# Decode states of a hybrid decoder step, stepped four tokens a unit and multiplied in eight pieces of four tokens

## The chip, the core and the metric

The kernel runs on one core of one Trainium2 chip. The metric is device time in microseconds (us) of one execution, the median of several. Of the core's engines, TensorE (PE in the profile, with its weight loads as PEld) does all matrix products, VectorE (DVE) and ScalarE (ACT) do elementwise work and empty PSUM, GpSimd (POOL) mostly issues the stores, and SyncE (SP) issues the loads. In the trace each engine's instructions come in the order of its own list; an instruction whose operand isn't ready holds what stands behind it there.

## The reference

One layer, with a prompt of 1024 tokens and eight decode tokens (`DEC_BATCH = 8`, one new token each). Both go through one input projection, then an RG-LRU group and an mLSTM group with four heads, then the output projection and a norm. What the change touches is the mLSTM of the decode tokens. For one decode token b and head h, with a state matrix C of 256 x 256 in float32:

```python
num = (jnp.einsum('bhts,bshv->bthv', P, v)
       + ginter.transpose(0, 2, 1)[..., None] * jnp.einsum('bthk,bhkv->bthv', q, C))
...
decay = jnp.exp(b[:, :, -1:] - b + igh - mL[:, :, None])
carry_scale = jnp.exp(b[:, :, -1] + m - mL)
C_new = carry_scale[..., None, None] * C + jnp.einsum('bhs,bshk,bshv->bhkv', decay, k, v)
```

So each of the 32 states (8 tokens x 4 heads, 256 KB each) is read, scaled by one number, given a rank-one update k v^T, and written out as an output. The kernel multiplies the token's query with the updated state (q C), and that product goes on into the token's output row.

## The kernel before

**The projection and its units.** The input projection is worked in 14 units of two blocks of 256 weight columns each (`UNITS`, unit 0 = `v0v1` to unit 13 = `z2z3`). A unit's two blocks against the two halves of the prompt make a 2 x 2 block product, which is done with seven products instead of eight (P1, P2, P5, P6, P7, P4, P3, by the names in the code), and each product in two halves. That makes 14 **parts** a unit. A part is twelve matmuls of 512 columns or twenty-four of 256, always in threes (`mm3`, lines 66 to 68: high x high, low x high, high x low of numbers that were split into a high and a low float32r part; the split is line 72 on ACT and line 73 on DVE). The weights of a product are prepared two products ahead of their use (`LEAD = 2`). Units 1 to 13 run from about 76 us to 667 us of the span; the output projection follows.

**The decode rows of a unit.** The decode tokens need the same projection. `dec_unit(u)` does it in float32 with eight matmuls (line 256) whose stationary operand is 32 columns wide; four of them stand side by side in the array, each at its own 32 columns (`pz[32 * g:32 * g + 32, :]`). It is issued where unit u's product P5 is prepared, which is just ahead of the unit's first part. ACT copies the result out (line 259), and a transposition follows later (line 264).

**The decode states.** When a head's q, k and v are there, its steps are queued in `dcq`: `first`, then `token(0)` to `token(7)`. A token's step scales its state on ACT (line 992), adds the rank-one update with two DVE instructions (line 994), has POOL store the state (line 996), and asks SP for the next token's v (line 965) and for later states (line 971). There are four state buffers (`Cb`, `bufs=4`). After each second token, `products` is put off by two parts (two passes through the `late` list) and then issues four matmuls for the two tokens: two halves of the state, two tokens, four 32-column places side by side in one PSUM bank (line 1013). These use a stationary operand of 32 columns for the first two tokens of a head (`qfirst`) and of 4 columns for the others (`qsel`). After the last two tokens DVE copies the bank (line 1019), and a small matmul pair (line 1024) sorts the rows.

**What sets the order.** After each part the loop calls `pop_bg`, which runs what is due in `late`, then takes a step each from the background work (`bg`), the RG-LRU steps (`rgq`), and, only at some parts, the decode steps (`dcq`). Before, that was each third part up to unit 9, and each second part from unit 10. The framework then orders the instructions of each engine itself: an instruction whose operands it reckons ready earlier can be put ahead of ones that the program lists first. So ACT's scaling of a state, which needs only the loaded state, often stands well ahead of the step's place in the loop. When the decode steps and all other background work are done after unit 9, the first blocks of the prompt's mLSTM (`m_first`) begin to be taken from `bg`.

Of the kernel before, what the change touches and what calls it, by code (L numbers as in the profile page):

```python
# [20 lines left out]
NB = 8  # L21
# [21 lines left out]

UNITS = "v0v1 x0y0 q0k0 x1y1 q1k1 x2y2 v2v3 q2k2 x3y3 q3k3 o0o1 o2o3 z0z1 z2z3".split()
NWS, NSTG, LEAD = 6, 7, 2
DEC = 10, 2, 3
RQ = [Q_P1, Q_P2, Q_P5, Q_P6, Q_P7, Q_P4, Q_P3]
NR, NZ = 28, 4

# [2 lines left out]
def hymba_kernel(  # L52
# [181 lines left out]
    def load_raw(u, b, parts=(0, 1)):  # L234
# [5 lines left out]
        for a in parts:  # L240
# [7 lines left out]
               "z": lambda j: dz[:, 2 * j:2 * j + 2], "x": lambda j: dxz[:, 0, 2 * j:2 * j + 2],  # L248
               "y": lambda j: dxz[:, 1, 2 * j:2 * j + 2]}

    def dec_unit(u):

        pz = ps("tr" if u < 2 else "o", [P, 512])
        for k in range(KC):
            g = k % 4
            TE.matmul(pz[32 * g:32 * g + 32, :], hnd[:, NB * k:NB * k + 32], raws[u, k // 4][:, k % 4, :], start=k < 4, stop=k >= 4,  # L256
                      skip_group_check=True)
        Z = sg([P, 512], "Z")
        A.copy(Z, pz)

        def turn():
            pt = ps("tr", [P, 4, P]) if u < 2 else pz.rearrange("p (m q) -> p m q", m=4)
            for m in range(4):
                TE.transpose(pt[:, m, :], Z[:, m * P:(m + 1) * P], idF)  # L264
            for a, (kind, j) in enumerate(units[u]):
                src = pt[:, 2 * a:2 * a + 2].rearrange("p m (g b) -> p m b g", g=4)[:, :, 0:NB, :]
                V.tensor_reduce(dec_dst[kind](j), src, axis=mybir.AxisListType.X, op=ALU.add)
                if kind == "k":
                    V.tensor_scalar(dec_dst[kind](j), dec_dst[kind](j), 1.0 / 16.0, None, op0=ALU.mult)
        late.append(turn if u < 2 else lambda: late.append(turn))  # L270
# [678 lines left out]

    def dec_open():  # L950
        p2 = fpr["p"]
        fetch_C(0)
        fetch_C(1)

        fpr["qsel"] = qsel = p2.tile([P, 2, 36], F32, tag="qsel", name="qsel")
        G.memset(qsel, 0.0)
        fpr["qfirst"] = qfirst = p2.tile([P, 2, 2, 32], F32, tag="qfirst", name="qfirst")
        G.memset(qfirst, 0.0)
        fpr["selq"] = selq = p2.tile([P, NB], F32, tag="selq", name="selq")
        idq = idF.rearrange("p (r k m) -> p r k m", r=2, k=2)  # L960
        V.tensor_tensor(selq.rearrange("p (m r) -> p r m", r=2), idq[:, :, 0, 0:4], idq[:, :, 1, 0:4], op=ALU.add)
# [11 lines left out]
    def decode_steps(h):  # L973

        p2 = fpr["p"]
        qsel, qfirst, selq = fpr["qsel"], fpr["qfirst"], fpr["selq"]
        st = {}

        def first():
            st["kw"] = kw = p2.tile([P, 2, NB], F32, tag="kw", name="kw")  # L980
            V.tensor_tensor(kw, dk[:, 2 * h:2 * h + 2, :], dW[:, :, h].unsqueeze(1).to_broadcast([P, 2, NB]), op=ALU.mult)
            V.tensor_copy(qsel.rearrange("p k (m r) -> p k m r", r=9)[:, :, :, 0:5:4],
                          dq[:, 2 * h:2 * h + 2, :].rearrange("p k (m r) -> p k m r", r=2))
            V.tensor_copy(qfirst[:, :, :, 0], dq[:, 2 * h:2 * h + 2, 0:2])
            fetch_v(h, 0)

        def token(b):
            i = h * NB + b

            def f():  # L990
                vb_, C = ds_.pop(("v", i)), ds_["C", i]
                A.mul(C, C, dGI[:, b, h:h + 1])
                for kb in range(2):
                    V.scalar_tensor_tensor(C[:, kb, :], vb_, st["kw"][:, kb, b:b + 1], C[:, kb, :],
                                           op0=ALU.mult, op1=ALU.add)
                stq(s_C[0, b, h].rearrange("(kb p) v -> p kb v", p=P), C)
                if b + 1 < NB:
                    fetch_v(h, b + 1)
                if b % 2:
                    late.append(lambda: late.append(products))  # L1000
                else:
                    fetch_C(i + 2)
                    fetch_C(i + 3)


            def products():
                if b == 1:
                    st["pq"] = ps("qp", [P, 512])
                pq = st["pq"]
                for g in range(4):  # L1010
                    bb, kb = b - 1 + g // 2, g % 2
                    q, n = (qfirst[:, kb, bb, :], 32) if b == 1 else (qsel[:, kb, 4 * bb:4 * bb + 4], 4)
                    TE.matmul(pq[32 * g:32 * g + n, 0:256], q, ds_["C", h * NB + bb][:, kb, :], start=b == 1,  # L1013
                              stop=b == NB - 1, skip_group_check=True)
                for bb in (b - 1, b):
                    del ds_["C", h * NB + bb]
                if b == NB - 1:
                    Z = sg([P, 256], "qC")
                    V.tensor_copy(Z, pq[:, 0:256])

                    def turn():
                        pt = pq[:, 256:272].rearrange("p (v b) -> p v b", v=2)
                        for vb in range(2):
                            TE.matmul(pt[:, vb, :], Z[:, vb * P:(vb + 1) * P], selq, start=True, stop=True)
                        V.tensor_copy(dqC[:, 2 * h:2 * h + 2, :], pt)
                    late.append(lambda: late.append(turn))
            return f
        return [first] + [token(b) for b in range(NB)]


    def bh(t):
# [660 lines left out]
    for n, (u, q) in enumerate(seq):  # L1692
        preps(n + 1 + LEAD)
        for _ in product(u, q):
            pop_bg(2 if u == 1 or u == last_u else 1, 1, part % DEC[1 if u >= DEC[0] else 2] == 1)
            part += 1
        if u == last_u:
            wo_due(q)
        if q == 6:
            for kind, j in units[u]:  # L1700
                if kind == "x":
                    rg_unit(j)
            for half in range(2):
                if u == max(unit_of["v", 2 * half], unit_of["v", 2 * half + 1], 1):
                    bg.append(lambda half=half: dec_rows(half))
            for h in range(NH):
                if done_h[h] == u:
                    bg.append(lambda h=h: dcq.extend(decode_steps(h)))
            if u == last_u - 1:
                dgen = decode_outputs()  # L1710

                def step():
                    next(dgen, None)
                    run_late()
                state["out"] = [step] * 5 + [m_open2]
        if not state["m"] and u > max(done_h) and not (bg or rgq or dcq or late):
            m_start()
        if u == last_u and q == 0:
            if not state["m"]:
                while bg or rgq or dcq or late:  # L1720
                    pop_bg()
                m_start()
            bg.extend(state["out"])
# [105 lines left out]
```

## Time and profile before

| what | value |
|---|---|
| time, median of 3 runs | 916.23 us (916.17 to 916.24) |
| profiled execution: span from first to last instruction | 913.5 us |
| median of the runs less that span | 2.7 us |
| PE busy / PEld / DVE / ACT / POOL | 902.1 / 749.2 / 741.5 / 590.1 / 194.2 us |
| mean granted TensorE clock | 0.998 |
| decode-row passes, line 256 | 224, in 14 groups of 16 |
| state-product passes, line 1013 | 128, in 16 groups of 8, first at 186.6 us, last at 538.0 us |

A float32 matmul stands in the trace as two passes, so eight matmuls are 16 rows there and four are 8. The profile gives only the span as the profiled execution's own time; what lies outside (2.7 us) is the launch and the end. In the timeline a row has its start, its length, engine, line, operation, output and inputs, tile shape, and a count. A matmul's length contains its way through the array and overlaps with its neighbours', so the cost of a stretch of TensorE work is read from starts, not from lengths.

### The profile page before, as it was taken

Reading aid. Unit: us, or ns where it says so; the run is one execution under the profiler, and the core shown is the slowest. Engines: PE = TensorE matmul, PEld = TensorE weight load, DVE = VectorE, ACT = ScalarE, POOL = GpSimd, SP = SyncE. Lnnn points to the kernel's source line nnn. Section 1 sums busy time; section 2 is a strip of 40 time slices with the busy share of each in tenths; the row PEclk is TensorE's granted clock in tenths of the full one; section 3 lists DMA queues with packets and bytes.
Section 4 is the critical chain, followed back from the end, with each engine's and each line's share of the span. In section 5 each row is a group of like instructions: output and inputs, shape, how many; then the busy total and the mean of one; then the engine's idle time right before and its main releaser. Section 6 shows DMA issues by size and latency. Waiting matters only on the chain.

```text
span 913.5 us, 15513 instructions
## 1 busy us (share of the span) xinstructions
PE 902.1 (99%) x5259; PEld 749.2 (82%) x5259; DVE 741.5 (81%) x1532; ACT 590.1 (65%) x1086; POOL 194.2 (21%) x322
## 2 busy tenths in 40 slices
PE   8999999999999999999999999999999999999996
PEld 6897777877787988787789898877788888888886
DVE  6874788978689878789888786679998879888973
ACT  7663446867567776577658786446786568566642
POOL 1111113112312222324332334010111111121120
PEclk9999999999999999999999999999999999999999
DMA  6611457455746566548665747345789889846531
GB/s 202 193 62 46 138 170 243 134 201 186 229 152 212 165 198 198 192 144 265 202 237 167 266 139 243 108 132 188 217 230 260 201 206 300 225 138 183 181 123 68
DMA packets 130488, 167.68 MB, mean 184 GB/s; under 512 B 17596, under 2 KB 98564, under 8 KB 130402
## 3 DMA queue, kind: packets, MB, share of 16 engines
q1 hardware_dynamic: 108790, 103.68, 37.4%
q0 software_dynamic: 21616, 63.02, 21.0%
q8 instruction: 41, 0.67, 0.3%
q14 instruction: 37, 0.30, 0.1%
q10 hardware_dynamic: 4, 0.00, 0.0%
HBM read 108.00 MB, written 62.92 MB: 187 GB/s over the span
## 4 chain that ended last, share of the span: by engine, by line
PE 97%; ACT 1%; DVE 1%; DMA 0%; issue 0%; POOL 0%; ACTq 0%; POOLq 0%
PE ps_o L66 16%; PE ps_o L68 15%; PE ps_o L67 15%; PE ps_kv L66 12%; PE ps_kv L68 11%; PE ps_kv L67 11%; PE ps_o L256 2%; PE ps_s L1195 2%; PE ps_qp L1013 1%; PE ps_s L824 1%; PE ps_tr L824 1%; PE ps_qp L67 1%; PE ps_qp L66 1%; PE ps_qp L68 1%; PE ps_s L1197 1%; PE ps_o L264 1%
## 5 line engine op out<-in xcount | busy, mean ns | idle before, releaser
L72 ACT CAST wh<-raw 128x1024 fp32r<-128x1024 f32 x91 | 95.4, 1049 | 77.9 <-PE ps_o L67 19.3
L73 DVE TENSOR_TENSOR wl<-raw,wh 128x1024 fp32r<-128x1024 f32 x91 | 111.0, 1220 | 34.9 <-ACT wh L72 19.8
L66 PE MATMUL ps_kv<-cb_hi,wh 128*128 128x512 f32 x320 | 127.3, 398 | 0.0
L68 PE MATMUL ps_kv<-cb_hi,wl 128*128 128x512 f32 x320 | 125.3, 392 | 0.0
L67 PE MATMUL ps_kv<-cb_lo,wh 128*128 128x512 f32 x320 | 125.0, 391 | 0.0
L66 PE MATMUL ps_o<-cb_hi,wh 128*128 128x512 f32 x240 | 95.2, 397 | 0.0
L68 PE MATMUL ps_o<-cb_hi,wl 128*128 128x512 f32 x240 | 93.7, 391 | 0.0
L67 PE MATMUL ps_o<-cb_lo,wh 128*128 128x512 f32 x240 | 93.6, 390 | 0.0
L66 PEld LDWEIGHTS ps_kv<-cb_hi,wh 128*128 128x128 f32 x320 | 60.1, 188 | 22.3 <-issue 4.6
L68 PEld LDWEIGHTS ps_kv<-cb_hi,wl 128*128 128x128 f32 x320 | 60.1, 188 | 13.0
L67 PEld LDWEIGHTS ps_kv<-cb_lo,wh 128*128 128x128 f32 x320 | 60.1, 188 | 12.7 <-issue 0.8
L66 PE MATMUL ps_kv<-wh,cb_hi 128*128 128x256 f32 x192 | 55.1, 287 | 0.0
L67 PE MATMUL ps_kv<-wl,cb_hi 128*128 128x256 f32 x192 | 54.4, 283 | 0.0
L68 PE MATMUL ps_kv<-wh,cb_lo 128*128 128x256 f32 x192 | 54.3, 283 | 0.0
L68 PEld LDWEIGHTS ps_o<-cb_hi,wl 128*128 128x128 f32 x240 | 45.1, 188 | 9.9
L66 PEld LDWEIGHTS ps_o<-cb_hi,wh 128*128 128x128 f32 x240 | 45.1, 188 | 9.7 <-issue 0.8
L66 PE MATMUL ps_o<-wo,mh 128*128 128x512 f32 (+1 forms) x136 | 53.0, 390 | 0.0
L67 PEld LDWEIGHTS ps_o<-cb_lo,wh 128*128 128x128 f32 x240 | 45.2, 188 | 8.9
L68 PE MATMUL ps_o<-wo,ml 128*128 128x512 f32 (+1 forms) x136 | 51.7, 380 | 0.0
L67 PE MATMUL ps_o<-wo,mh 128*128 128x512 f32 (+1 forms) x136 | 51.5, 379 | 0.0
L66 PE MATMUL ps_o<-wh,cb_hi 128*128 128x256 f32 x144 | 41.0, 285 | 0.0
L67 PE MATMUL ps_o<-wl,cb_hi 128*128 128x256 f32 x144 | 40.7, 283 | 0.0
(560 smaller groups left out, 2599.8 us busy)
## 6 DMA issues: line engine op xcount, KB each, us to landing
raw<-in_w_in_dram SPq DMA_DIRECT2D x55, 512.0 KB
Cb<-in_state_mlstm_C_dram SPq DMA_DIRECT2D x32, 256.0 KB
out_dram<-Cb POOLq DMA_DIRECT2D x32, 256.0 KB, 4.5
qk<-d_qk SPq DMA_DIRECT2D x32, 256.0 KB
ring<-d_ro SPq DMA_DIRECT2D x26, 256.0 KB
d_qk<-s POOLq DMA_DIRECT2D x24, 256.0 KB, 4.9
d_x<-s POOLq DMA_DIRECT2D x16, 256.0 KB, 2.8
zsr<-d_y SPq DMA_DIRECT2D x16, 256.0 KB
```

What stands on the lines that cost most here:

```text
L66: TE.matmul(out, ah, bh, start=first, stop=False, skip_group_check=True)
L67: TE.matmul(out, ah, bl, start=False, stop=False, skip_group_check=True)
L68: TE.matmul(out, al, bh, start=False, stop=last, skip_group_check=True)
L72: a = A.copy(hi, src)
L73: V.tensor_tensor(lo, src, hi.bitcast(F32), op=ALU.subtract)
L256: TE.matmul(pz[32 * g:32 * g + 32, :], hnd[:, NB * k:NB * k + 32], raws[u, k // 4][:, k % 4, :], start=k < 4, stop=k >= 4, skip_group_chec ...
L264: TE.transpose(pt[:, m, :], Z[:, m * P:(m + 1) * P], idF)
L824: TE.matmul(pg, w[:, n, :], st["xx"][n], start=k == 0, stop=k == 1)
L1013: TE.matmul(pq[32 * g:32 * g + n, 0:256], q, ds_["C", h * NB + bb][:, kb, :], start=b == 1, stop=b == NB - 1, skip_group_check=True)
L1195: TE.matmul(S, qk[:, 2 + kb, :], qk[:, kb, :], start=kb == 0, stop=kb == 1)
L1197: TE.transpose(kn[:, kb * P:(kb + 1) * P], qk[:, 2 + kb, :], idF)
```

## The change

Three things are changed together.

- **When the steps run.** The decode steps are taken at the parts 3, 5, 7, 9 and 11 of every unit (`DEC`), in place of each third or each second part. A head now takes two units: `first` and tokens 0 to 3 in one, an empty step and tokens 4 to 7 in the next.
- **When the products run.** They are issued for four tokens at a time, eight matmuls, eight times in all. After a group's fourth token, the group is put into a list `full`; the next `dec_unit` issues it right behind its own eight matmuls.
- **When the states are loaded.** Four states are fetched at the opening, and then four at a time, two parts after a group's products, into the same four buffers. Before, two were fetched at every second token.

```diff
-DEC = 10, 2, 3
+DEC = 3, 5, 7, 9, 11
...
+    full = deque()
+
     def dec_unit(u):
...
             TE.matmul(pz[32 * g:32 * g + 32, :], hnd[:, NB * k:NB * k + 32], raws[u, k // 4][:, k % 4, :], start=k < 4, stop=k >= 4,
                       skip_group_check=True)
+        if full:
+            full.popleft()()
         Z = sg([P, 512], "Z")
         A.copy(Z, pz)
...
-        fetch_C(0)
-        fetch_C(1)
+        for i in range(4):
+            fetch_C(i)
...
-                if b % 2:
-                    late.append(lambda: late.append(products))
-                else:
-                    fetch_C(i + 2)
-                    fetch_C(i + 3)
-
+                if b % 4 == 3:
+                    full.append(products)
 
             def products():
-                if b == 1:
+                if b == 3:
                     st["pq"] = ps("qp", [P, 512])
                 pq = st["pq"]
-                for g in range(4):
-                    bb, kb = b - 1 + g // 2, g % 2
...
+                for b0 in (b - 3, b - 1):
+                    for g in range(4):
+                        bb, kb = b0 + g // 2, g % 2
+                        q, n = (qfirst[:, kb, bb, :], 32) if b0 == 0 else (qsel[:, kb, 4 * bb:4 * bb + 4], 4)
+                        TE.matmul(pq[32 * g:32 * g + n, 0:256], q, ds_["C", h * NB + bb][:, kb, :], start=b0 == 0,
+                                  stop=b0 == NB - 2, skip_group_check=True)
+                for bb in range(b - 3, b + 1):
                     del ds_["C", h * NB + bb]
+                for n in (1, 3):
+                    late.append(lambda n=n: late.append(lambda: [fetch_C(i + n), fetch_C(i + n + 1)]))
...
-        return [first] + [token(b) for b in range(NB)]
+        steps = [token(b) for b in range(NB)]
+        return [first, *steps[:4], lambda: None, *steps[4:]]
...
-            pop_bg(2 if u == 1 or u == last_u else 1, 1, part % DEC[1 if u >= DEC[0] else 2] == 1)
+            pop_bg(2 if u == 1 or u == last_u else 1, 1, part % 14 in DEC)
```

**TensorE, the start of unit 4, before.** `raw0_4` and `raw1_4` are the unit's weights with the decode tokens as stationary operand (`hnd`); `ps_kv` is the first part's output.

```order
L256 MATMUL ps_o_2217<-raw0_4_1943,hnd_112 32x512 x4
L256 MATMUL ps_o_2217<-raw1_4_2057,hnd_112 32x512 x4
L66 MATMUL ps_kv_2234<-cb_hi0_187,wh4_0_2118 128x512
L67 MATMUL ps_kv_2234<-cb_lo0_188,wh4_0_2118 128x512
...
L68 MATMUL ps_kv_2234<-cb_hi0_187,wl4_0_2119 128x512
L1013 MATMUL ps_qp_2077<-Cb_1935,qsel_1374 4x256 x2
L1013 MATMUL ps_qp_2077<-Cb_1937,qsel_1374 4x256 x2
L66 MATMUL ps_kv_2260<-cb_hi0_187,wh4_0_2118 128x512
L67 MATMUL ps_kv_2260<-cb_lo0_188,wh4_0_2118 128x512
```

**The same place in the change.**

```order
L258 MATMUL ps_o_2208<-raw0_4_1937,hnd_112 32x512 x4
L258 MATMUL ps_o_2208<-raw1_4_2057,hnd_112 32x512 x4
L1014 MATMUL ps_qp_2217<-Cb_1370,qfirst_1380 32x256 x2
L1014 MATMUL ps_qp_2217<-Cb_1372,qfirst_1380 32x256 x2
L1014 MATMUL ps_qp_2217<-Cb_1374,qsel_1378 4x256 x2
L1014 MATMUL ps_qp_2217<-Cb_1376,qsel_1378 4x256 x2
L66 MATMUL ps_kv_2234<-cb_hi0_187,wh4_0_2109 128x512
L67 MATMUL ps_kv_2234<-cb_lo0_188,wh4_0_2109 128x512
```

The pieces that stood apart among the projection's matmuls are now one group behind the decode rows, with nothing between. The other seven groups stand the same way, behind the decode rows of units 5, 6, 7, 9, 10, 11 and 12.

**ACT, the start of unit 4, before.** `Z` is the copy of the decode rows, `s1` the copy of the first product's halves, `Cb` the scaling of a state, `wh4_3` and `wh4_4` high parts of the weights of later products.

```order
L259 COPY Z_2226<-ps_o_2217 128x512
L330 COPY s1_2247<-ps_kv_2234 128x512
L811 CAST xl_2284<-xc_2256 64x512
L992 ACTIVATE Cb_2294<-Cb_2294,dGI_110 128x512
L330 COPY s1_2273<-ps_kv_2260 128x512
L72 CAST wh4_3_2299<-raw0_4_1943 128x1024
L992 ACTIVATE Cb_2296<-Cb_2296,dGI_110 128x512
L72 CAST wh4_4_2345<-raw0_4_1943 128x1024
```

**The same place in the change.**

```order
L263 COPY Z_2226<-ps_o_2208 128x512
L334 COPY s1_2247<-ps_kv_2234 128x512
L815 CAST xl_2288<-xc_2252 64x512
L996 ACTIVATE Cb_2271<-Cb_2271,dGI_110 128x512
L996 ACTIVATE Cb_2273<-Cb_2273,dGI_110 128x512
L996 ACTIVATE Cb_2275<-Cb_2275,dGI_110 128x512
L334 COPY s1_2269<-ps_kv_2256 128x512
L72 CAST wh4_3_2293<-raw0_4_1937 128x1024
L996 ACTIVATE Cb_2277<-Cb_2277,dGI_110 128x512
L72 CAST wh4_4_2339<-raw0_4_1937 128x1024
```

Four scalings of states now stand close behind the decode rows, three of them ahead of the second `s1` copy. Their buffers are the ones that the products of the same unit have just read, so their loads can only be issued once those products are done.

**TensorE, unit 12, the prompt's first mLSTM block, in the change.** `ps_s<-qk` are its scores, `kh`, `vh`, `vl`, `ph` the operands that ACT and DVE make from them, `ps_o_6138` the projection's second half of P2.

```order
L1199 MATMUL ps_s_6009<-qk_5965 128x128 x2
L1201 MATMUL ps_s_6009<-idF_78,qk_5965 128x128 x2
L68 MATMUL ps_o_6138<-cb_hi1_189,wl12_1_5915 128x512
...
L66 MATMUL ps_qp_6098<-vh_5953,kh_6017 128x258
...
L66 MATMUL ps_s_6102<-vh_5953,kh_6017 128x258
...
L67 MATMUL ps_qp_6098<-vl_5954,kh_6017 128x258
...
L66 MATMUL ps_qp_6132<-vh_5953,ph_6015 128x258
...
L1199 MATMUL ps_s_6165<-qk_5971 128x128 x2
```

Before, the scores stood ahead of unit 12's decode rows, and 24 matmuls of the projection lay between them and the first use of `kh`. In the change the scores come some 40 rows later and five matmuls lie between. After this block the order of TensorE is the same as before to the end.

More of the change, by code (lines that the diff above doesn't have):

```diff
@@ L998, in f @@
                     fetch_v(h, b + 1)
-                if b % 2:
-                    late.append(lambda: late.append(products))
-                else:
-                    fetch_C(i + 2)
-                    fetch_C(i + 3)
+                if b % 4 == 3:
+                    full.append(products)
             def products():
-                if b == 1:
+                if b == 3:
                     st["pq"] = ps("qp", [P, 512])
                 pq = st["pq"]
-                for g in range(4):
-                    bb, kb = b - 1 + g // 2, g % 2
[L1012 to L1015, printed above, removed]
+                for b0 in (b - 3, b - 1):
[5 more added lines that the diff above has]
+                for bb in range(b - 3, b + 1):
                     del ds_["C", h * NB + bb]
+                for n in (1, 3):
+                    late.append(lambda n=n: late.append(lambda: [fetch_C(i + n), fetch_C(i + n + 1)]))
                 if b == NB - 1:
```

## The prediction

> **What bounds the kernel now.** I read the page first, then the table by stretches, TensorE's timeline around one group of the rows that the change moves, and last the waits.
>
> ```profile
> span 913.5 us, 15513 instructions
> PE 902.1 (99%) x5259; PEld 749.2 (82%) x5259; DVE 741.5 (81%) x1532; ACT 590.1 (65%) x1086; POOL 194.2 (21%) x322
> ```
> ```profile
> 112.00:612.00 500.00, 500.00 (x2911) 411.09 (x2913) 408.97 (x712) 336.07 (x498) 133.93 (x214) 1.00 0.59 190
> ```
>
> The second row is the stretch that holds all the work in question (units 2 to 13): PE is busy in 500 of 500 us at full clock, DVE in 409, ACT in 336, the DMA engines in 59% at 190 GB/s. A busy PE alone proves little, since the lengths of its rows overlap. So I look at starts.
>
> ```profile
> 205.63 0.40 PE L67 MATMUL ps_kv<-cb_lo,wh 128*128 128x512 f32 x1
> 205.87 0.39 PE L68 MATMUL ps_kv<-cb_hi,wl 128*128 128x512 f32 x1
> 206.10 0.40 PE L66 MATMUL ps_kv<-cb_hi,wh 128*128 128x512 f32 x1
> 206.33 0.39 PE L67 MATMUL ps_kv<-cb_lo,wh 128*128 128x512 f32 x1
> 206.56 0.39 PE L68 MATMUL ps_kv<-cb_hi,wl 128*128 128x512 f32 x1
> 206.88 0.61 PE L1013 MATMUL ps_qp<-Cb,qsel 128*4 128x256 f32 x8
> 207.43 0.50 PE L66 MATMUL ps_kv<-cb_hi,wh 128*128 128x512 f32 x1
> 207.76 0.39 PE L67 MATMUL ps_kv<-cb_lo,wh 128*128 128x512 f32 x1
> 207.99 0.40 PE L68 MATMUL ps_kv<-cb_hi,wl 128*128 128x512 f32 x1
> ```
>
> Full-size matmuls start every 0.23 us and nothing delays them; only around the product piece does the step widen, before it, behind it, and once more after the first full-size matmul. TensorE sets the time here, and each us of its stream saved is a us of span, as long as no other engine falls behind. [...]
>
> **The price of a piece.** From the last full-size start before (206.56) to the second one after (207.76) are 1.20 us; two steps would take 0.46. So this piece of two tokens costs 0.74 us. The same reading for a first piece of a head (32 columns) and for the decode rows of a unit:
>
> ```profile
> 186.32 0.39 PE L68 MATMUL ps_kv<-cb_hi,wl 128*128 128x512 f32 x1
> 186.64 0.64 PE L1013 MATMUL ps_qp<-Cb,qfirst 128*32 128x256 f32 x8
> 187.55 0.39 PE L67 MATMUL ps_kv<-cb_lo,wh 128*128 128x512 f32 x1
> ```
> ```profile
> 157.79 0.39 PE L68 MATMUL ps_kv<-cb_hi,wl 128*128 128x512 f32 x1
> 158.11 1.92 PE L256 MATMUL ps_o<-raw,hnd 128*32 128x512 f32 x16
> 159.96 0.50 PE L66 MATMUL ps_kv<-cb_hi,wh 128*128 128x512 f32 x1
> 160.30 0.40 PE L67 MATMUL ps_kv<-cb_lo,wh 128*128 128x512 f32 x1
> ```
>
> They cost 187.55 - 186.32 - 0.46 = 0.77 us and 160.30 - 157.79 - 0.46 = 2.05 us. Now both kinds run four passes side by side. A product piece is 8 passes of 256 columns, two rounds; the decode rows are 16 passes of 512 columns, four rounds of double length. With r for a round of 256 columns and s for going over to these narrow tiles and back: 2r + s = 0.74 and 8r + s = 2.05. So r = 0.218 us and **s = 0.30 us**. That s is the change of tile shape, and not of float32, is seen where one 128-wide float32 transposition stands inside the decode rows of unit 2:
>
> ```profile
> 115.20 0.39 PE L68 MATMUL ps_kv<-cb_hi,wl 128*128 128x512 f32 x1
> 115.52 1.06 PE L256 MATMUL ps_o<-raw,hnd 128*32 128x512 f32 x8
> 116.59 0.33 PE L701 MATMUL ps_qp<-idF,stk 128*128 128x128 f32 x1
> 116.85 1.06 PE L256 MATMUL ps_o<-raw,hnd 128*32 128x512 f32 x8
> 118.18 0.39 PE L67 MATMUL ps_kv<-cb_lo,wh 128*128 128x512 f32 x1
> ```
>
> This stretch costs 118.18 - 115.20 - 0.46 = 2.52 us, 0.47 more than the same rows without it, for a transposition of a quarter of the columns of a full-size matmul.
>
> **The sum on TensorE.**
>
> ```profile
> L1013 PE MATMUL ps_qp<-Cb,qsel x96: 379/379/380, 206.9 to 538.0; 128*4 128x256 f32 x96
> L1013 PE MATMUL ps_qp<-Cb,qfirst x32: 379/391/403, 186.6 to 497.4; 128*32 128x256 f32 x32
> ```
>
> - Removed: 12 pieces at 0.74 and 4 at 0.77, 11.96 us. Two of them stand directly ahead of another narrow or square float32 group and share the way back; I take off 0.15. Remains 11.8.
> - Added: 8 groups behind the decode rows. Each is 16 passes of 256 columns, four rounds: 4 x 0.218 = 0.87 us, with no s, because the decode rows have already paid it. The four with a `qfirst` take 0.03 more. Together 7.1 us.
> - Net: **-4.7 us**. The streaming is the same on both sides, 32 rounds; what goes is sixteen changes of shape and back, 16 x 0.30 = 4.8.
>
> What the trace doesn't hold is a round of narrow float32 tiles that follows a round on other data in another PSUM bank, nor one of 4 columns behind one of 32. Its bounds: nothing (as between rounds of one piece), and a full s at each of the eight seams, 8 x 0.30 = 2.4 us, which would leave -2.3. I take nothing: decode rows and pieces both start four passes at once, so both already work in the same four 32-column places. [...]
>
> **The other moved parts.** The scalings, updates, stores and loads of the 32 states stay in number; only their places change.
>
> - *Products waiting for their states.* TensorE now takes eight matmuls in a fixed place, and all of the projection is queued behind them. In DVE's order at least 24 rows lie between the last update of a group and the subtraction (line 285) that DVE does right behind the decode rows. By the stretch above a DVE row takes 409 / 712 = 0.57 us, so the updates are done some 13 us ahead; against that DVE runs a few us behind TensorE. I price it at nothing. Without that cover it would be up to a token's two updates, about 1 us, a group.
> - *ACT waiting for loads.* This is the wait that the change reshapes.
>
> ```profile
> ACT Cb L992 <- DMA Cb<-in_state_mlstm_C_dram: 22.8, 13, 3.5
> SPq L971 <- PE ps_qp L1013: 44.3, 11, 6.9
> ```
> ```profile
> 474.71 0.90 SPq L971 DMA_DIRECT2D Cb<-in_state_mlstm_C_dram  x2
> ```
> ```profile
> 480.96 0.72 ACT L992 ACTIVATE Cb<-Cb,dGI 128x512 f32<-128x512 f32 x1 [3.53 <-DMA Cb<-in_state_mlstm_C_dram]
> 481.58 0.57 ACT L330 COPY s<-ps_kv 128x512 f32<-128x512 f32 x1
> 482.05 1.04 ACT L72 CAST wh<-raw 128x1024 fp32r<-128x1024 f32 x1
> 483.00 0.72 ACT L992 ACTIVATE Cb<-Cb,dGI 128x512 f32<-128x512 f32 x1
> ```
>
> ACT waits 22.8 us in 13 places for states now, at worst 6.2 us after the issue (474.71 to 480.96), and the second state of that pair was there 8.3 us after it at the latest. TensorE had no gap there. In the change four states are asked for right behind the products, seven times (the first four come early). The 512 KB more take 2.8 us at 190 GB/s, so the fourth state lands at most L = 11 us after the products. Behind it on ACT stand its scaling (0.72), a copy (0.57) and a split (1.04), then DVE's half of that split (1.2, line 73 in the page):
>
> ```profile
> L73 DVE TENSOR_TENSOR wl<-raw,wh 128x1024 fp32r<-128x1024 f32 x91 | 111.0, 1220 | 34.9 <-ACT wh L72 19.8
> ```
>
> TensorE wants that weight for the fourth product, six parts of 12 x 0.23 = 2.76 us in, at 16.5 us. So L may be 16.5 - 3.5 = 13 us; at 11 two us are left. I price it at nothing.
> - *The prompt's first block.* It begins some ten us later in unit 12 and its chain (scores, ACT, DVE, products) has five matmuls, 1.15 us, as cover where it had 24. ACT's two pieces there take about 0.47 and 0.40 us:
>
> ```profile
> 560.41 0.40 ACT L72 CAST vh<-vt 128x256 fp32r<-128x256 f32 x1
> ...
> 564.62 0.47 ACT L1203 ACTIVATE kh<-ps_s,de_t 128x256 fp32r<-128x256 f32 x1
> ```
>
> They just fit. I put +0.2 us, between 0 and 1 (all of 0.87 in the open).
>
> Sum: -4.7 + 0.2 = -4.5 us. The span goes from 913.5 to about 909.0, and with the 2.7 us around it the time from 916.23 to **911.7 us**.
>
> **The rivals.**
>
> 1. *The seams cost a change of shape after all*, once a group: 8 x 0.30 = 2.4 us given back, 914.1 us. For it: 4-column tiles have never followed 32-column ones here. Against it: both start four at a time and overlap, which needs the same places.
> 2. *Side waits eat part of it*: in some units ACT or DVE is late by one or two us, or the prompt's block costs its full 1 us. 1 to 2.5 us in all, 912.7 to 914.2 us. For it: ACT's 3.5 us waits. Against: in 500 us of the present kernel they cost TensorE nothing.
> 3. *Nothing comes of it*, 916.2 us: TensorE's stream isn't the bound, or the saved changes are filled by waits that now show. DVE is next in line with 409 of the 500 us, 91 us of room against 4.5, so this needs waits, not work.
> 4. *Slower, by ACT.* Four loads in a burst land later than L = 13 us, ACT stands, and the fourth product's weights are late in each of the seven units: TensorE loses 7 x (L - 13). From L = 13.6 the gain is gone, from 13.9 the kernel is over 0.2% slower; at L = 14.5, 911.7 + 10.5 = 922 us. For it: all four share one SP queue with the weights of the next unit, and the stores of four states come in a burst too. Against: the slowest pair had 8.3 us at most.
>
> **How the numbers follow.** A measurement of this kernel can tell 0.2%, 1.8 us, from no change. Chances: the forecast 0.70, rival 1 0.10, rival 2 0.10, rival 3 0.06, rival 4 0.04. The forecast, rival 1 and nearly all of rival 2 lie under 914.4, so faster 0.87, same 0.09, slower 0.04. The range: at the low end the net sum with the present ACT waits gone where they might have cost something, -5.7, 910.5 us; at the high end the full price of the seams, 914.1, so that rivals 3 and 4 and a little more are left out.
>
> **What would show it.** In the profile of the changed kernel: line 1014 in 8 groups of 16 passes, each directly behind line 258, and from the last full-size start before such a pair to the second one behind it 2.05 + 0.87 + 0.46 = 3.4 us; with the seam's price it would be 3.7. TensorE busy without gaps from 112 us to 607. ACT's wait for states between 10 and 40 us in total, no single one over 7. The prediction is wrong if TensorE shows waits for ACT, DVE or states at line 66 or 1014 that add to over 2 us, or if the span shrinks by more than the removed changes of shape (5 us), which would mean that something else in the stretch was paid for.

## The result and the profile after

The change takes **917.43 us** (median of 21 runs) against 915.99 us for the kernel before on the same chip. The ratio is 1.0016, with a 95% interval of 1.001 to 1.0021: no gain, and 1.4 us lost where 4.5 were to be saved. One of the 21 runs took 2285.6 us, for which nothing here shows a reason, and is left out of the ratio; the other twenty lie further apart, from 915.7 to 919.8 us, than those of before, from 915.1 to 916.6.

The page's first lines of the changed kernel, from an execution that took 917.50 us, and its row for the stretch of units 2 to 13 (columns as in the prediction: PE, PEld, DVE, ACT, POOL, granted clock, DMA share, GB/s):

```profile
span 915.6 us, 15488 instructions
PE 900.3 (98%) x5259; PEld 753.2 (82%) x5259; DVE 741.3 (81%) x1532; ACT 590.6 (65%) x1086; POOL 195.1 (21%) x322
```
```profile
112.00:612.00 500.00, 496.93 (x2896) 414.31 (x2895) 407.93 (x710) 335.62 (x496) 134.16 (x213) 0.99 0.59 190
```

PE is no longer busy in all of the 500 us, and the clock's mean in them fell from 1.00 to 0.99. Both come from one place, shown below. First, what went as planned, TensorE's timeline around the first group, behind the decode rows of unit 4:

```profile
201.00 0.39 PE L68 MATMUL ps_kv<-cb_hi,wl 128*128 128x512 f32 x1
201.32 1.92 PE L258 MATMUL ps_o<-raw,hnd 128*32 128x512 f32 x16
203.06 0.61 PE L1014 MATMUL ps_qp<-Cb,qfirst 128*32 128x256 f32 x8
203.49 0.61 PE L1014 MATMUL ps_qp<-Cb,qsel 128*4 128x256 f32 x8
204.04 0.50 PE L66 MATMUL ps_kv<-cb_hi,wh 128*128 128x512 f32 x1
204.37 0.40 PE L67 MATMUL ps_kv<-cb_lo,wh 128*128 128x512 f32 x1
```

From the last full-size start before to the second one behind are 204.37 - 201.00 = 3.37 us; the prediction had 2.05 + 0.87 + 0.46 = 3.38, and 3.7 with a price at the seam. The seam is free, also from 32 columns to 4 (203.49 - 203.06 = 0.43, two rounds of 0.216). By unit 10 TensorE is 3.2 us ahead of before. Its decode rows there, before and in the change:

```profile
469.15 1.06 PE L256 MATMUL ps_o<-raw,hnd 128*32 128x512 f32 x8
```
```profile
465.97 1.92 PE L258 MATMUL ps_o<-raw,hnd 128*32 128x512 f32 x16
```

There the lead ends. TensorE's timeline in unit 10, where P6 ends and P7's first half begins:

```profile
493.88 0.28 PE L68 MATMUL ps_kv<-wh,cb_lo 128*128 128x256 f32 x1
497.05 0.58 PE L66 MATMUL ps_kv<-wh,cb_hi 128*128 128x256 f32 x1 [2.89 <-ACT s L344]
497.43 0.41 PE L67 MATMUL ps_kv<-wl,cb_hi 128*128 128x256 f32 x1
497.64 0.41 PE L68 MATMUL ps_kv<-wh,cb_lo 128*128 128x256 f32 x1
```

The step is 3.17 us where 0.12 was usual. P7's first half adds into the PSUM bank whose content after P6 must first be copied out (`s2`, line 344); ACT is late with that copy. Behind the stall the matmuls start 0.21 us apart instead of 0.12. The table by stretches says why, in the column of the granted clock (last but two):

```profile
480.00:494.00 14.00, 14.00 (x117) 13.86 (x115) 9.27 (x18) 11.74 (x17) 3.58 (x5) 1.00 0.58 180
497.00:503.00 6.00, 5.95 (x28) 5.95 (x29) 5.80 (x12) 5.10 (x9) 2.28 (x4) 0.51 0.19 65
503.00:510.00 7.00, 7.00 (x59) 6.91 (x59) 4.80 (x7) 3.21 (x5) 3.97 (x6) 1.00 0.92 261
```

For some 6 us TensorE runs at half clock: 28 matmuls start where 6 us at 0.12 us would hold 50. That is 28 x 0.093 = 2.6 us more. Stall and clock together, 3.05 + 2.6 = 5.6 us, are more than the whole saving. The unit takes 52.0 us, from its decode rows to the next unit's, where it takes 46.3 in the run without this stall (e3, below).

Why was ACT late? DVE's and ACT's timelines ahead of it:

```profile
456.60 0.88 DVE L998 SCALAR_TENSOR_TENSOR Cb<-vbc,kw,Cb 128x256 f32<-128x256 f32 x2 [3.86 <-DMA vbc<-d_dv]
...
482.90 0.88 DVE L998 SCALAR_TENSOR_TENSOR Cb<-vbc,kw,Cb 128x256 f32<-128x256 f32 x2
484.29 0.87 DVE L998 SCALAR_TENSOR_TENSOR Cb<-vbc,kw,Cb 128x256 f32<-128x256 f32 x2
487.12 0.88 DVE L998 SCALAR_TENSOR_TENSOR Cb<-vbc,kw,Cb 128x256 f32<-128x256 f32 x2 [1.96 <-DMA vbc<-d_dv]
487.92 0.68 DVE L337 TENSOR_TENSOR s<-s,ps_o 128x512 f32<-128x512 f32 x1
```
```profile
474.44 1.05 ACT L72 CAST wh<-raw 128x1024 fp32r<-128x1024 f32 x1 [3.07 <-DVE raw L286]
...
480.06 0.73 ACT L996 ACTIVATE Cb<-Cb,dGI 128x512 f32<-128x512 f32 x1 [1.95 <-DMA Cb<-in_state_mlstm_C_dram]
...
488.63 0.63 ACT L384 ACTIVATE s<-s 128x512 f32<-128x512 f32 x1 [1.81 <-DVE s L337]
...
495.89 0.63 ACT L850 ACTIVATE na<-na 128x512 f32<-128x512 f32 x1
496.43 0.57 ACT L344 COPY s<-ps_kv 128x512 f32<-128x512 f32 x1
```

Three loads hold it. In unit 9 a token's v (`vbc`) lands at 456.60, after DVE has stood 3.86 us for it; DVE then works without a gap of note to 480 us, and ACT's first weight split of unit 10 (474.44) waits 3.07 us for it. The fourth state lands at 480.06. And another v lands at 487.12: DVE stands 1.96 us for it with the sum of line 337 behind, ACT's tanh (line 384) waits for that sum, and behind the tanh ACT works without a gap to the copy that TensorE waits for. The four tokens, which the loop takes two parts apart (2 x 12 x 0.23 = 5.5 us), stand close together on both engines: the last three updates lie within 5.1 us. The parts don't set the engines' order; the framework takes a step as soon as it reckons its buffer free and its load landed. The waits of the stretch 112 to 612 us in total, times and longest, DVE's for v before, then those of the change:

```profile
DVE Cb L994 <- DMA vbc<-d_dv: 4.0, 3, 3.5
```
```profile
DVE Cb L998 <- DMA vbc<-d_dv: 14.8, 8, 3.9
ACT Cb L996 <- DMA Cb<-in_state_mlstm_C_dram: 6.5, 5, 2.8
PE ps_kv L66 <- ACT s L344: 2.9, 1, 2.9
```

DVE's wait for v grew from 4.0 to 14.8 us. ACT's wait for states fell from 22.8 to 6.5 us, and yet the kernel lost: the sum of an engine's waits doesn't say which of them somebody waits for.

### The profile page after: what moved, and what is told of

Read it like the earlier page. It is cut to its first block, busy times and chain, and to the rows that moved or that the text cites. A ratio compares the mean times of both kernels' runs of the same rounds, so it can differ in the third digit from the quotient of the medians.

```text
span 915.6 us, 15488 instructions
## 1 busy us (share of the span) xinstructions
PE 900.3 (98%) x5259; PEld 753.2 (82%) x5259; DVE 741.3 (81%) x1532; ACT 590.6 (65%) x1086; POOL 195.1 (21%) x322
## 4 chain that ended last, share of the span: by engine, by line
PE 83%; DVE 7%; DMA 4%; ACT 3%; issue 2%; POOL 0%; SPq 0%; DVEq 0%; ACTq 0%; POOLq 0%
PE ps_o L66 13%; PE ps_o L68 13%; PE ps_o L67 13%; PE ps_kv L66 10%; PE ps_kv L67 9%; PE ps_kv L68 9%; PE ps_o L258 2%; PE ps_s L1199 2%; DMA vbc<-d_dv 1%; DMA Cb<-in_state_mlstm_C_dram 1%; DVE wl L73 1%; PE ps_qp L66 1%; PE ps_qp L67 1%; PE ps_qp L68 1%; PE ps_s L1201 1%
## 5 line engine op out<-in xcount | busy, mean ns | idle before, releaser
L998 DVE SCALAR_TENSOR_TENSOR Cb<-vbc,kw,Cb 128x256 f32<-128x256 f32 x64 | 28.0, 479 | 18.2 <-DMA vbc<-d_dv 14.8
L66 PEld LDWEIGHTS ps_kv<-wh,cb_hi 128*128 128x128 f32 x192 | 38.0, 198 | 4.8 <-ACT s L344 3.3
```

The costliest lines, as they stand in the source:

```text
L66: TE.matmul(out, ah, bh, start=first, stop=False, skip_group_check=True)
```

## The experiments

Three theories were set against each other. **T1**: the v loads, with two buffers, hold DVE. **T2**: the four states loaded in one burst hold ACT. **T3**: ACT and DVE in units 9 to 11 have next to no slack against TensorE, so that any lead of TensorE is lost there, whatever brought it.

Ratios are to the kernel before on the same chip, with their 95% intervals.

| run | median us | ratio |
|---|---|---|
| e1 the change again | 917.99 | 1.0024 (1.001 to 1.0037) |
| e2 change, four v buffers | 913.78 | 0.9973 (0.9961 to 0.9985) |
| e3 change, one state | 911.67 | 0.9952 (0.994 to 0.9965) |
| e4 before, no products | 934.65 | 1.0204 (1.019 to 1.0218) |
| e5 before, short products | 916.55 | 1.0002 (0.9993 to 1.0011) |
| e6 scalings held | 921.5 | 1.0057 (1.0044 to 1.007) |
| e7 scalings held, four v | 913.88 | 0.997 (0.9958 to 0.9982) |
| e8 before, four v | 916.28 | 1.0003 (0.9994 to 1.0012) |
| e9 four v, held from unit 10 | 912.98 | 0.9958 (0.9946 to 0.997) |
| e10 before, one state | 915.93 | 0.9994 (0.9985 to 1.0003) |
| e11 short products, one state | 913.37 | 0.9972 (0.9959 to 0.9985) |
| e12 short products, four v | 915.89 | 0.9997 (0.9985 to 1.001) |
| e13 v loads by GpSimd | 940.44 | 1.0256 (1.0234 to 1.0278) |
| e14 four v, held but in unit 9 | 914.34 | 0.9978 (0.9969 to 0.9988) |
| e15 as e14, v loads by GpSimd | 919.55 | 1.0031 (1.0019 to 1.0043) |
| e16 state loads by GpSimd | 925.51 | 1.0099 (1.0083 to 1.0114) |

### The change once more (e1)

> The changed kernel as it is, profiled a second time. All theories below take the stall in unit 10 for the cause: TensorE waits 2 to 4 us at line 66 for ACT's copy at line 344 between 490 and 500 us, and the granted clock halves for some 7 us behind it. If the second profile shows that, the time is again 916 to 919 us. If it is another place that loses the time in this execution, the loss isn't one late copy but small slack everywhere, and the theories are too narrow.

The second profile (span 918.5 us) has the same stall in the same unit, 3.2 us with the clock halved for 3.4 us behind it, and four more of 0.6 to 1.1 us, at 133, 318, 475 and 489 us. TensorE's waits in it:

```profile
PE ps_kv L66 <- ACT s L344: 4.0, 2, 3.0
PE ps_o L66 <- DVE s L337: 1.4, 3, 0.7
PE ps_kv L66 <- ACT c L359: 0.9, 1, 0.9
```

So in both profiles the loss is mainly the one late copy, but other handoffs lie within a us of being late too, and in some executions are. That fits the wider spread of the change's runs. It isn't shown for every execution: of the twenty runs in the result, eleven have a mean clock of 0.995 or 0.996 (0.995 in the profiled one, 0.998 in the profile of before), but five have 0.998 or 0.999, and three of these took 919.1 to 919.8 us. What they lose can hardly be half clock, and no trace shows where it goes.

### Four v buffers (e2, and e8 as control)

```diff
-        ... tag="vbc", name="vbc", bufs=2)
+        ... tag="vbc", name="vbc", bufs=4)
```

> The change with four buffers for a token's v instead of two; the order on TensorE and ACT is word for word the change's. Theory T1 (DVE is held by v loads, since four tokens now stand close together and only two v's fit; behind DVE's update stands the sum that ACT's tanh needs, behind that the copy that TensorE waits for): DVE's waits for v fall from 14.8 us to under 3, ACT's wait for DVE near 488 us goes, TensorE's stall near 495 us shrinks from 3.05 to under 1.2 us, the clock isn't halved, time 911.5 to 913.5 us. T2 (ACT is held by the four states loaded in a burst): nothing changes, 917 us. T3 (ACT's and DVE's work of units 9 and 10 has its own pace with about 1 us of slack, so what TensorE gains ahead of it is lost there): the stall stays at 2 us or more, 916 to 917.5 us.

> The kernel before with four v buffers: control for the second run. All theories: TensorE had no gap there, so nothing changes, 915.5 to 916.5 us. If it gains over 1 us, the v loads cost something before as well and the gain of four buffers is no part of the change.

DVE's waits for v fall to 0.4 us, ACT's first split of unit 10 starts at 472.90 instead of 474.44, and the time is 4.2 us under that of the change on the same chip (e1), if 0.3 us above T1's range. In the kernel before the same edit moves nothing. T1 is right as far as it goes, but two stalls of a us stay in unit 10 at the same copy, now behind ACT's waits for states:

```profile
PE ps_kv L66 <- ACT s L344: 1.8, 2, 1.0
```
```profile
477.55 0.72 ACT L996 ACTIVATE Cb<-Cb,dGI 128x512 f32<-128x512 f32 x1 [1.88 <-DMA Cb<-in_state_mlstm_C_dram]
479.68 0.72 ACT L996 ACTIVATE Cb<-Cb,dGI 128x512 f32<-128x512 f32 x1 [1.41 <-DMA Cb<-in_state_mlstm_C_dram]
```

### No state loads (e3, and e10 as its partner)

```diff
-            ds_["C", i] = t = ...tile([P, 2, 256], F32, tag="Cb", name="Cb", bufs=4)
-            ld(t, st_C[0, b, h]...)
+            ds_["C", i] = ...tile([P, 2, 256], F32, tag="Cb", name="Cb", bufs=4)
...
-                A.mul(C, C, dGI[:, b, h:h + 1])
+                A.mul(C, fpr["cst"], dGI[:, b, h:h + 1])
```

> The change without the reads of the 31 other states: every scaling on ACT reads one resident state and writes the token's buffer, so no state load is waited for; all else on TensorE is as in the change (the decode outputs are therefore of one state). T1: DVE still waits for v, the stall in unit 10 stays over 2 us, time 915.5 to 917.5 us. T2: no ACT wait, no stall, 911.5 to 913 us. T3: ACT is 2 us less late, the stall shrinks to about 1 us, 913 to 915.5 us.

> The kernel before without the reads of the 31 other states (scalings read one resident state; the decode outputs are of one state), order on TensorE word for word that of before. Loads as the anchor, and TensorE the bound of before: no gap there that a load could close, so 915.3 to 916.4 us; against the third run (the change without state reads, 911.67) that leaves the sum on TensorE, 4 to 4.7 us. If the time falls below 914.5, state loads hold back the kernel before as well, and the third run's gain was theirs and not that of the moved products.

Without state loads the change takes 911.67 us, the kernel before 915.93: no state load holds before back (e10), and **the sum on TensorE is real: 4.3 us** by the medians, 3.8 by the ratios (0.9952 / 0.9994), against the 4.5 of the prediction. In the two traces TensorE takes 4.5 us less in e3 from unit 3's decode rows to unit 13's (158.62 to 607.35 us, against 158.65 to 611.85). In e3 ACT makes the copy of unit 10 some 5 us earlier (496.43 in the change), although that unit starts at 466.0 us in both:

```profile
468.36 0.72 ACT L997 ACTIVATE Cb<-cst,dGI 128x512 f32<-128x512 f32 x1 [0.29 <-PE ps_qp L1015]
...
491.26 0.57 ACT L344 COPY s<-ps_kv 128x512 f32<-128x512 f32 x1
```

Of these 5.2 us, 2.8 are there at the unit's first weight split already (471.63 us, against 474.44). Three of the four scalings now run from 468 to 471 us, ahead of that split. In the changed kernel all four stand behind it, while ACT is idle 3.07 us ahead of it. ACT's order is the framework's, which puts ahead what it reckons ready earlier: so a load can cost more than its own wait, by putting work out of an idle stretch of ACT into a full one. DVE still waits 10.7 us for v in e3, without harm. So with waits for v alone (e3) TensorE has no wait between 112 and 612 us, with waits for states nearly alone (e2) two of a us, and the 3 us stall takes both. By the ratios four v buffers bring the kernel 2.5 us under the one before, no state loads 4.4. (TensorE's order in e3 is that of the change, and in e10 that of before, but ACT's and DVE's are not, and 8 MB of reads are gone, so the other loads may land sooner; e3 doesn't separate these from the waits.)

### Less work on TensorE, nothing moved (e4, e5, e11, e12)

e4 leaves the product matmuls of the kernel before out, and the sorting pair behind them. e5 keeps them in their places and shortens them (DVE's copy of the bank then reads its 64 columns four times):

```diff
-                    TE.matmul(pq[32 * g:32 * g + n, 0:256], q, ds_["C", ...][:, kb, :], ...
+                    TE.matmul(pq[32 * g:32 * g + n, 0:64], q, ds_["C", ...][:, kb, 0:64], ...
```

e11 is e5 with the state edit of e3, e12 is e5 with four v buffers.

> The kernel before with all product pieces left out (the decode values computed from the states are therefore missing; states are stepped and stored as ever, at the places of before). TensorE has 11.8 us less to do, some 10 us of it ahead of unit 10's end. T1 and T2: the steps stand as before, no stall, 916.0 - 11.8 = 904.2, range 903.5 to 905.5 us. T3: TensorE reaches unit 10's copies early and waits there for ACT 5 us or more, with the clock halved behind it; 908 to 913 us.

> The kernel before with every product piece cut to 64 of a state's 256 columns, in its old places: the order of the loads is untouched, 32 rounds of 0.218 us fall to a quarter or a little more, so TensorE has 4 to 5 us less, 3.5 us of it ahead of unit 10's end, as in the change (the decode values are therefore wrong). If the loss in the change comes from TensorE running ahead of ACT and DVE, whatever the order of the steps (T3), it appears here too: TensorE waits over 2 us for ACT's copies in units 9 and 10, the clock is halved behind it, 914.5 to 917 us. If it needs the change's burst of four loads, scalings and v's right behind the decode rows (T2 and T1), nothing waits here: 911 to 912.5 us.

e4 lost 18.7 us with 11.8 us less to do. It isn't the test it was meant to be: with nothing left that reads the states on TensorE, a buffer comes free with its store, and the framework put the next load right behind that. SP then stood for stores, and ACT for the loads, at worst 5.9 us:

```profile
SPq L971 <- DMA out_dram<-Cb: 54.7, 23, 5.7
```
```profile
146.72 1.40 ACT L992 ACTIVATE Cb<-Cb,dGI 128x512 f32<-128x512 f32 x2 [5.88 <-DMA Cb<-in_state_mlstm_C_dram]
148.15 0.59 ACT L340 COPY s<-ps_kv 128x512 f32<-128x512 f32 x1
```

e5 leaves the orders of the loads and of TensorE alone, and is the plain test of T3. (With the shorter pieces the framework moved some rows on ACT and DVE, on ACT none between 450 and 520 us, where the first two waits below lie.) Each of its pieces costs 0.42 to 0.45 us instead of 0.74 to 0.77, 16 x 0.32 = 5.1 us in all, and **the time stays the same**. At unit 10 TensorE is 3.6 us ahead; at unit 12 it is 0.3 us ahead. The lead went in TensorE's waits of units 10 and 11, without half clock:

```profile
PE ps_kv L66 <- ACT c L355: 1.7, 1, 1.7
PE ps_s L930 <- ACT dxc L920: 1.5, 1, 1.5
PE ps_kv L66 <- ACT s L340: 0.9, 1, 0.9
```

So T3 holds, and for the kernel before: it has no gap on TensorE, and no room for a lead either. Whether ACT's and DVE's own work leaves no room, or the loads that they wait for, e11 asks.

> Products cut to 64 columns in their old places, as in the fifth run, and no state reads, as in the tenth. If the landing of loads is what keeps ACT from following TensorE, the 5.1 us that the fifth run lost now arrive: 910.3 to 911.8 us, and TensorE has no wait for ACT in units 9 to 11. If ACT's and DVE's own work sets the pace there (T3 in its narrow form), 914 to 916 us.

> The fifth run with four v buffers instead of two. There ACT's copy at line 340 was late behind a DVE wait for v (1.85 us at 485.58), and the copy at line 355 behind a state load (4.07 us at 461.47). If each load is a cause of its own, the first stall (1.1 us) goes and the second (1.7 us) stays: 914 to 915.8 us. If v is all, 911 to 912.5; if neither, 916.5.

In e11 TensorE has no wait for ACT in unit 10 any more and comes to unit 11 at 512.8 us, against 517.4 in e10: 4.6 us ahead, so there it was the loads, or the later places that they have in ACT's list, and not the amount of ACT's own work. Then, in the profiled execution, it meets the next load. The RG-LRU's last transpositions (line 930) have a fixed place in TensorE's order and wait for ACT and DVE, and DVE stands for a small array of the prompt's first block:

```profile
555.54 0.35 DVE L1176 SCALAR_TENSOR_TENSOR We<-W,be_t,maskT 128x128 f32<-128x128 f32 x1 [4.66 <-DMA W<-d_alpha]
```

TensorE waits 3.2 us, the clock halves for 3.4 us, and unit 12 starts at 564.4 us against 565.0. This execution took 916.70 us and is one of two of the twelve with a mean clock under 0.997; the other ten took 912.2 to 914.8 us. The median shows 2.6 of the 5.1 us, between the two ranges. In e12 the wait for the copy at line 340 is gone and the one at line 355 stays (1.8 us), as the expectation had it, and the one at line 930 grows to 2.4; the time, 0.1 us above its range, can't be told from that of e5. In the kernel before, v is the smaller part of what TensorE's lead runs into.

### Spreading the steps (e6, e7, e9, e14)

`issue_after` puts an instruction behind another one in its engine's order, without a wait. e6 holds each scaling behind the last copy that ACT made for the projection, e7 adds four v buffers, e9 does both and holds only from unit 10 on, e14 in all units but 9. The framework orders the rest anew around the held rows, some of TensorE's too.

```diff
-            A.copy(t, X)
+            held[:] = [A.copy(t, X)]
...
-                A.mul(C, C, dGI[:, b, h:h + 1])
+                with tc.issue_after(held[0].ins):
+                    A.mul(C, C, dGI[:, b, h:h + 1])
```

> The change with each state's scaling put on ACT behind the copy (lines 335 to 360) that ACT last made before the token's own part, so that the four scalings of a group stand apart over the second half of a unit instead of right behind the decode rows; two v buffers as in the change, loads as soon as buffers come free. If the burst is the cause (T2, with T1 as its second half, since the v's are then wanted one by one too): ACT's wait for states under 2 us, DVE's for v under 5, no TensorE wait over 1 us in units 9 and 10, 911.5 to 912.5 us. If it is only the number of v buffers (T1 alone): v waits stay above 10 us, 914 to 917 us. T3: stall of 2 us or more stays, 915.5 to 917.5 us.

> The same with four v buffers. Burst theory: no further gain over the same with two, 911.4 to 912.5 us. T1: here and not there the stall goes, 911.5 to 913.5 us against 914 to 917.

Spreading takes ACT's waits for states away in e6 and e7 (none is left among its waits), but with two v buffers (e6) it is the slowest of these four, and slower than any theory had it. There the fourth token's v is issued at 503.34 us, right behind two weight loads of 512 KB, and is used at 514.63:

```profile
502.32 0.94 SPq L243 DMA_DIRECT2D raw<-in_w_in_dram  x2
503.34 13.11 SPq L970 DMA_DIRECT2D vbc<-d_dv  x3
```
```profile
514.63 0.48 DVE L1000 SCALAR_TENSOR_TENSOR Cb<-vbc,kw,Cb 128x256 f32<-128x256 f32 x1 [6.87 <-DMA vbc<-d_dv]
```

Behind that update stands the sum of line 352, ACT is idle 8.18 us for it, and TensorE waits for ACT's copy at line 358, with half clock for 3.4 us behind it:

```profile
PE ps_kv L66 <- ACT c L358: 3.8, 1, 3.8
```

Between e6 and e7 lie 7.6 us for two v buffers. So T2 alone is wrong: with the burst gone, v is later than ever. And e7 gains no more than e2: its unit 10 is 2.3 us shorter (46.3 against 48.6), but its unit 9 is 3.4 us longer (47.0 against 43.6). Part of that isn't loss: two RG-LRU matmuls (line 829) that end unit 8 in e2 stand behind the decode rows of unit 9 in e7, where TensorE waits 0.6 us for DVE.

> The change with four v buffers, and the scalings held to their parts only in units 10 and later, where the second run still lost 2.1 us in two stalls, and left free before, where the seventh run lost some 3 us in unit 9. If each loss stays in its own unit, both are gone: unit 10 takes about 46.3 us as in the seventh run, time 911.4 to 912.6 us. If TensorE's lead only runs into the next late copy, as T3 has it, 913 to 914.5 us.

> The ninth run with the scalings held to their parts in all units but 9. By the two runs' unit lengths, held units 6 and 8 are 1.3 and 0.4 us shorter than free ones (45.9 against 47.2, 42.1 against 42.5 us), and held unit 9 is 2.8 us longer. If each unit keeps its own length, 911.2 to 912.0 us. If the lead runs into the next late handoff instead, 912.6 to 914 us.

e9 has the lowest median of the kernels that compute everything: 912.98 us, 3.0 us under the kernel before and 4.4 under the change (its interval overlaps those of e2 and e7). Unit 10 takes 46.3 us, as expected, and the time falls between the two ranges. One stall of 1.2 us is left, in unit 6:

```profile
PE ps_kv L66 <- ACT s L345: 1.3, 2, 1.1
```

e14 was put together from the unit lengths of two runs, and missed: 914.34 us. Its unit 9 took 46.6 us, as held, though it was left free: the two matmuls of line 829 stand in it as in e7, and in e9 they don't. The unit lengths that were added held different work; lengths of units from different orders don't add.

### Other queues (e13, e15, e16)

The v loads (e13, e15) or the state loads (e16) are issued by GpSimd:

```diff
-        ld(t, d_dv[h][b:b + 1, :]...)
+        stq(t, d_dv[h][b:b + 1, :]...)
```

> The change with its two v buffers, the v loads issued by GpSimd, which otherwise issues the stores, instead of SP; the order on TensorE and ACT is word for word the change's. If v is late because it stands behind states and weights in SP's queue, DVE's waits for v fall from 14.8 us to under 5 and the time to 913 to 915 us. If it is late because there are two buffers (a load can't be issued before the update two tokens back, and then takes some 3 us), the waits stay at 10 us or more and the time at 916.5 to 918.5 us.

> The same, v loads issued by GpSimd. With four buffers no v is waited for, whatever the queue: within 0.5 us of the fourteenth run. If GpSimd issues them late behind waiting stores, DVE waits again and it is 1 us or more slower.

> The change with the state loads issued by GpSimd instead of SP (two v buffers). If states are late because of what else SP's queue carries, ACT's waits for states (6.5 to 11.9 us in the two profiles of the change) fall under 3 us and the time to 913.5 to 916 us. If the four loads take their time on any queue, or wait behind stores, 916.5 us or more.

All three lose, e13 far outside both of its ranges. In e13 the v's come later still: in GpSimd's list the next v stands behind a token's store, and the store waits for that token's update:

```profile
374.23 0.72 POOL L1000 DMA_DIRECT2D out_dram<-Cb  x1 [7.42 <-DVE Cb L998]
374.94 0.55 POOL L969 DMA_DIRECT2D vbc<-d_dv  x1
```

That neither clears nor blames SP's queue, but it gives a third point on the effect of late v's, with ACT's and TensorE's orders those of the change:

```profile
DVE Cb L998 <- DMA vbc<-d_dv: 42.2, 13, 7.2
```

DVE waits for v 0.4, 14.8 and 42.2 us in e2, the change and e13; the times are 913.8, 917.4 and 940.4 us. e15's expectation was wrong: with four buffers DVE waits for no v, and yet the kernel is 5.2 us slower than e14. In its profile TensorE waits 3.9 us for ACT and DVE, against 2.2 in e14, and DVE 10.1 us for the RG-LRU's inputs (`xs`), against 7.2; no run shows whether that is the cause. In e16 ACT still waits 11.0 us for states, as its second branch had it, and TensorE 9.4 us for ACT and DVE.

## Why the prediction was wrong

The prediction named what would show it wrong, TensorE's waits for ACT adding to over 2 us, and that is what the trace shows (2.9). Its steps in turn:

- **The sum on TensorE, -4.7 us: right.** A group costs 3.37 us where 3.38 was said. The seams, taken as free without a run that showed it, are free: in all eight groups the first round stands 0.43 us behind the decode rows' last, as their own rounds do, and each further one 0.216. Rival 1 is out, and e3 against e10 gives 3.8 to 4.3 us in time and 4.5 us between two places in the traces. The products wait for no update, as said.
- **"Each us of its stream saved is a us of span, as long as no other engine falls behind": this is where it failed.** The condition was taken for met, since TensorE had no gaps, and the side waits were priced at nothing. In the change they cost 5.6 us in unit 10. e5 shows that before the change ACT and DVE, with the loads they wait for, were already just in time in units 10 and 11: 5.1 us less on TensorE, in place, bring nothing. A row without gaps says that nobody is late, not how early they are. The prediction argued with DVE's 91 us of room in 500; room in a sum doesn't help where the order leaves none. Rival 3, at 0.06, comes closest, the saving filled by waits that now show; it stopped at 916.2 us.
- **ACT waiting for four loads, priced 0: the landing was right, the deadline wrong.** The fourth state was to land at most 11 us after the products. In unit 10 the products end at 466.0 + 2.9 = 468.9 us, and ACT uses that state at 480.06: 11.2 us. But the 13 us allowed came from one consumer, the weights of the fourth product. What came too late was another thing in ACT's list, the copy of P6 some 16 us further down, at the end of a full stretch. Rival 4 named the mechanism (ACT behind a burst) but not this place; it expected the loss in each of seven units, and the trace shows it in one. ACT's waits for states came to 6.5 us, under the 10 to 40 that were forecast, so their sum was no sign of it.
- **The v loads: left out.** The prediction counted the states' loads and not the tokens' v. With four updates close together, two buffers are too few: 14.8 us of DVE waits against 4.0 before, the longest of them in unit 9, and 4.2 us of time (e2 against e1).
- **A stall's price: left out.** The 3.05 us cost 5.6 us with the clock. The bounds of rivals 2 and 4 were worked out at full clock.
- **The prompt's first block, +0.2: about right.** Between 550 and 600 us the steps from one matmul of the projection to the next of the same shape exceed the usual 0.23 and 0.12 us by 0.6 us in all, against 0.4 before, and e3 against e10 gives the 4.5 us of the sum with this term in it.

Two things are not settled. One is where the executions with a mean clock of 0.998 or more lose their time. The other is how much of v's lateness is the buffers and how much SP's queue. e2 shows that buffers suffice in the change's order, e6 shows one v that took 11 us behind a MB of weights, and e13 doesn't tell them apart.

## What to carry to other kernels

Before a saving on the busiest engine is booked, find out how early its feeders are: shorten that engine's work in place, as in e5, and see whether the time follows. Where work is gathered into larger groups, every load that serves it is gathered too, the small ones with two buffers as well, and the deadline of a late load is the most urgent thing anywhere behind it in the waiting engine's list: here the copy of P6, some 16 us behind the fourth state's scaling.

## What the runs showed of the hardware

In these runs a long stall of TensorE cost more than its length: in the change the stall of 3.05 us in unit 10 came with 6.83 us at a granted clock of 0.5 (496.1 to 502.9 us), of which the 5.9 us behind the stall cost another 2.6 us. In the 18 profiles, between 100 and 660 us, all 12 stalls of 2.7 us or more (from start to start, less the usual step) were followed by a granted clock of 0.5; of the 10 between 1.78 and 2.6 us three were, of the shorter ones none. Among the twelve, half clock began 2.2 to 5.4 us after the last start ahead of the stall and lasted 3.41 us nine times and 6.83 us three times. So stalls of 2.7 us were enough each time, and one of 1.78 was; what decides between 1.78 and 2.6 us these runs don't show.

In the change's four groups with both kinds, narrow float32 tiles of 4 columns follow those of 32 columns without a price: a round starts 0.216 us behind the one before it, at the seam (203.28 to 203.49 us in unit 4) as within either kind. Going over from full-size matmuls and back, once for each piece, had cost 0.30 us before, by the prediction's reading of 0.74 us for a piece and 2.05 for the decode rows.
